# One decoder layer on one core: w_ada in pairs of blocks, the seam of the channel mixing in a pinned order, and operand tiles placed alike modulo 512 bytes

## The chip, the core and the metric

The kernel runs on one core of a Trainium2 chip. The metric is device time in microseconds (us) of one execution; of several executions the median is given. TensorE (PE) multiplies matrices, VectorE (DVE) and ScalarE (ACT) work on elements, GpSimd (POOL) does elementwise work and issues some transfers, and SyncE's queue (SP) issues most transfers (DMA). Matmul results stand in PSUM, everything else that an engine reads stands in SBUF, whose 128 partitions each hold a row of bytes; an address below is a byte offset in such a row.

## The reference

One conditioned decoder layer, in float32, on 1024 tokens of width 1024:

```
mod = silu(c) @ w_ada + b_ada                 # 1024 x 6144: shift1 scale1 gate1 shift2 scale2 gate2
h   = rmsnorm(x)*norm1_g*(1+scale1) + shift1
p   = h @ w_in                                # 5384 columns: r, wd, k, v, ad, gd | q, k, v, f | two gates
ya  = rwkv7(p ...); yb = forgetting_attention(p ...)
x   = x + gate1 * ((sigmoid(ga)*(ya@w_o_rwkv) + sigmoid(gb)*(yb@w_o_fox)) @ w_out)
h2  = rmsnorm(x)*norm2_g*(1+scale2) + shift2
x   = x + gate2 * (square(relu(h2 @ w_ff1)) @ w_ff2)      # 1024 -> 4096 -> 1024
y   = rmsnorm(x)*final_g
```

Every matrix product is computed to nearly float32 accuracy: an operand is split into a rounded part (`hi`, made by ACT) and the rest (`lo`, made by DVE as operand minus `hi`), and TensorE adds hi·hi, lo·hi and hi·lo. Such a product of 128x128 by 128x512 is three matmuls.

## The kernel before

The program is written engine by engine in Python; a scheduler orders the instructions of each engine ahead of time, by its own cost estimates, and inserts the semaphore waits. Tiles come from pools; a tile with a tag waits until the last reader of the tile that held the tag's buffer before it is done. Pools stand on the left or the right side of SBUF, and a pool that is opened where another was closed waits in the same way. `tc.keep_in_program_order` keeps an instruction in the order of the program on its engine, and `tc.issue_after(i)` lets instructions be put into the order only behind `i`.

**The start** (0 to 87 us). `x` comes in eight tiles of 128 tokens, all loaded first. `normalise(g)` squares four of them on ACT and scales them, the first four on DVE, the last four on ACT. scale1 and shift1 are 2 x 8 blocks of 128 numbers: `ada_load(k)` brings block k of both (two transfers of 0.5 MB, a run of 512 bytes per row of w_ada, three buffers), and `ada_sum(k)` multiplies row j by silu(c)[j] and adds up: three of the eight row groups on POOL, five on DVE, and a last sum over partitions on PE (matmuls of one column, `gp<-ones,acc`), which DVE turns into `gs`. `modulate(k)` transposes the 128 columns k of all eight `x` tiles on PE (`xp`), and ACT and DVE make `hhi`, `hlo` of them. `products(k)` then adds k's part to the first three projections, 18 matmuls of 128x512: `wa` (decay and in-context-lr columns), `r0` and `k0`. The order written is: `x`, wa block 0, the three weights, block 1; then k = 0 to 7, with sum and transposes one block ahead.

**The middle** (87 to 930 us) is the two mixers; the change does not touch it. **p_out** (930 to 1023 us) is the product with w_out, 384 matmuls of 128x512 `p_out<-h_wo,hhi` and the like (L1181 to L1192), with the residual and second norm.

**Channel mixing, up** (to 1351 us): w_ff1 goes in 16 pairs of columns; each pair is a 2x2 block product done in the 7 products of Winograd's form of Strassen's scheme, of 12 matmuls each. The operands made of h2 (`B11`, `B21`, `B22`, `T1` to `T4`) stay; those made of w_ff1 (`uwhi/uwlo`, `S1` to `S4`, `A22`) are made anew for each pair from a load `ur` (L1114). The results are squared, summed (`f_sum`) and written to a DRAM buffer `f_d`, in the seven combinations that the down product needs.

**Channel mixing, down** (1345 to 1670 us): 4 groups of 7 steps, 48 matmuls each. Step s takes one of the seven from `f_d` (`dA`, split into `dh` and `fl`) and one combination of four blocks of w_ff2 (`B11`, `B12`, `B21`, `B22`, scaled by gate2; split into `wh` and `wl`). Even and odd steps use two sets of four PSUM banks, `y` and `x`. `prepare(s+1)` makes the operands of the next step and `loads(s+3)` issues the transfers three steps ahead; `evict` adds a PSUM bank to the output sums `acc`.

**The seam** is the place where up ends and down begins. Step 0's operands (`da`, `db`, made to `dh`, `dl`) are prepared during the last pair, and its matmuls start before the last pair's `T4` product. Those of step 1 (A11, B11) need buffers of the pools `fr` and `fp`, which open only when the pools of the up stage are closed:

```
for name in ("S1", "S2", "S4"):
    f_sum(NPAIR - 1, name)
for stack in (hx[2], hx[0], dax, hx[1], mix):
    stack.close()
psum_pools(x=(4, 512), y=(4, 512))
with pool(name="fr", bufs=1, side="right") as fr, pool(name="fp", bufs=1) as fp:
```

In the order that results, DVE scales B22 (`B_0_11641` below), makes `fl` of step 1's dA (`dA_11633`) and only then scales B11 (`B_0_11634`); the split of B11 (ACT `wh`, L1099; DVE `wl`, L1100) and with it step 1 wait for that. The loads go in the order dA3, B22, dA1, B11, dA2, B12.

## Time and profile before

| | us |
|---|---|
| median of 3 runs (1678.31 to 1679.96) | 1678.47 |
| profiled execution | 1680.21 |
| its span, first to last instruction | 1678.5 |
| PE busy in the span | 1591.5 (95%) |
| DVE busy | 1132.0 (67%) |
| ACT busy | 730.7 (44%) |
| POOL busy | 357.9 (21%) |

The mean granted clock of TensorE over the profiled execution is 0.991 of full speed. Matmul times in a row are of a pipelined engine: one 128x512 matmul is shown with 0.39 us, but the next starts about 0.23 us after it. The distance from start to start (the pitch) is therefore what a matmul costs on a busy PE. In the chain of waits a piece "x48" is 48 instructions in a row on one engine, and its length over 48 is their pitch.

### The profile page before, as it was taken

To read this page: it belongs to the slowest core of one execution; us is meant where nothing else is said; L and a number is where in the kernel's file an instruction comes from. 1 tells how busy PE (TensorE), PEld (TensorE's weight loads), DVE (VectorE), ACT (ScalarE), POOL (GpSimd) and SP (SyncE) were. 2 spreads that over 40 slices of the span, in tenths; PEclk is the share of its full clock that TensorE was granted. 3 is DMA by queue.
4 is the path that set the end of the run, shared out by engine and by line. 5 is a ranking of instruction groups with operands and counts; after the bars stand their busy time and mean duration, and the time that the engine had idled before them with its cause. 6 is when DMAs were issued, how large, how long until landed. Compare 5 with 4: busy or idle time off the path is not lost.

```text
span 1678.5 us, 21911 instructions
## 1 busy us (share of the span) xinstructions
PE 1591.5 (95%) x8293; PEld 1274.8 (76%) x8293; DVE 1132.0 (67%) x1685; ACT 730.7 (44%) x1138; POOL 357.9 (21%) x362
## 2 busy tenths in 40 slices
PE   2989999999999999999999999999999979999997
PEld 1767777777777878888887787777777858888886
DVE  5777665657655736665737656975555579899978
ACT  5455343535454623332333234655545534433334
POOL 4310000899990011221110000122211110000000
PEclk9999999999999999999999999999999989999999
DMA  8525456422223178778767431344444474364422
GB/s 242 149 79 161 127 152 155 113 63 63 70 60 117 32 213 262 231 242 230 239 207 237 152 113 51 139 150 154 144 160 150 158 288 161 120 220 158 168 75 101
DMA packets 217111, 256.24 MB, mean 153 GB/s; under 512 B 30097, under 2 KB 156330, under 8 KB 216878
## 3 DMA queue, kind: packets, MB, share of 16 engines
q1 hardware_dynamic: 204094, 209.99, 41.3%
q0 software_dynamic: 12704, 44.57, 6.9%
q8 instruction: 65, 1.06, 0.3%
q14 instruction: 40, 0.33, 0.1%
q10 hardware_dynamic: 208, 0.28, 0.0%
HBM read 178.16 MB, written 72.45 MB: 149 GB/s over the span
## 4 chain that ended last, share of the span: by engine, by line
PE 70%; DVE 10%; DMA 7%; ACT 5%; issue 3%; SPq 0%; DVEq 0%; ACTq 0%
PE x L1221 18%; PE y L1221 11%; PE p_gb L41 5%; PE p_out L41 5%; PE p_ga L41 3%; PE p_ob L41 2%; PE p_fv L41 2%; DMA ur<-in_w_ff 2%; PE my L41 2%; PE p_fk L41 2%; PE p_fq L41 2%; PE z L1221 2%; PE p_v L41 2%; PE yv L41 2%; PE tp L825 2%
## 5 line engine op out<-in xcount | busy, mean ns | idle before, releaser
L1410 ACT CAST dh<-dA 128x1024 fp32r<-128x1024 f32 x54 | 56.4, 1046 | 139.9 <-PE x L1221 72.2
L1221 PE MATMUL x<-wh,dh 128*128 128x512 f32 x256 | 102.1, 399 | 9.4 <-ACT wh L1099 9.4
L645 POOL TENSOR_TENSOR dg<-dg,inv 128x62 f32<-128x62 f32 (+30 forms) x62 | 100.2, 1616 | 4.8
L1221 PE MATMUL x<-wl,dh 128*128 128x512 f32 x256 | 100.9, 395 | 0.0
L1221 PE MATMUL x<-wh,fl 128*128 128x512 f32 x256 | 100.1, 391 | 0.0
L644 POOL TENSOR_TENSOR inv<-dg 128x62 f32<-128x62 f32 (+30 forms) x62 | 92.8, 1497 | 4.9
L1591 DVE TENSOR_TENSOR fl<-dA,dh 128x1024 fp32r<-128x1024 f32 x54 | 65.1, 1218 | 16.1 <-ACT dh L1410 10.3
L1221 PE MATMUL y<-wh,dh 128*128 128x512 f32 x176 | 69.4, 394 | 0.0
L1221 PE MATMUL y<-wl,dh 128*128 128x512 f32 x176 | 68.6, 393 | 0.5 <-DVE wl L1100 0.5
L1221 PE MATMUL y<-wh,fl 128*128 128x512 f32 x176 | 68.3, 388 | 0.0
L829 DVE TENSOR_TENSOR pl<-tp,ph 128x512 fp32r<-128x512 f32 (+1 forms) x80 | 49.1, 631 | 24.9 <-ACT ph L828 24.6
L1221 PEld LDWEIGHTS x<-wh,dh 128*128 128x128 f32 x256 | 48.8, 191 | 19.6 <-ACT wh L1099 9.8
L885 DVE CUSTOM_DVE_ANT_0 pt<-s,cb 128x512 f32<-128x512 f32 (+2 forms) x64 | 36.4, 584 | 37.5 <-PE s L41 36.6
L887 ACT ACTIVATE pt<-pt,sm 128x128 f32<-128x128 f32 (+3 forms) x64 | 49.5, 775 | 24.4 <-DVE sm L885 23.4
L707 POOL TENSOR_TENSOR sw<-sbd,wcs 64x256 f32<-64x256 f32 x28 | 22.9, 816 | 167.9 <-DVE sbd L708 137.7
L1245 ACT ACTIVATE ff<-ff 128x512 f32<-128x512 f32 x48 | 30.3, 632 | 64.9 <-DVE ff L1331 29.5
L1221 PEld LDWEIGHTS x<-wl,dh 128*128 128x128 f32 x256 | 48.3, 189 | 12.0 <-DVE wl L1100 0.5
L1221 PEld LDWEIGHTS x<-wh,fl 128*128 128x128 f32 x256 | 48.6, 190 | 10.7
L828 ACT CAST ph<-tp 128x512 fp32r<-128x512 f32 (+1 forms) x80 | 41.6, 543 | 29.1 <-PE tp L825 27.2
L1236 POOL DMA_DIRECT2D f_d<-ff x48 | 25.9, 540 | 125.5 <-ACT ff L1246 121.1
L825 PE MATMUL tp<-ident,pt 128*128 128x128 f32 x288 | 49.6, 282 | 2.1 <-ACT pt L887 1.7
L41 PE MATMUL p_out<-h_wo,hhi 128*128 128x512 f32 x128 | 50.8, 397 | 0.6 <-ACT h_wo L1056 0.6
(586 smaller groups left out, 4932.6 us busy)
## 6 DMA issues: line engine op xcount, KB each, us to landing
dA<-f_d SPq DMA_DIRECT2D x27, 1024.0 KB
aw<-in_w_ada SPq DMA_DIRECT2D x32, 512.0 KB
ur<-in_w_ff SPq DMA_DIRECT2D x30, 512.0 KB
B<-in_w_ff SPq DMA_DIRECT2D x15, 1024.0 KB
f_d<-ff POOLq DMA_DIRECT2D x48, 256.0 KB, 4.3
wa<-in_w_ada SPq DMA_DIRECT2D x16, 512.0 KB
sc_d<-scb SPq DMA_DIRECT2D x16, 512.0 KB
sct<-sc_d SPq DMA_DIRECT2D x16, 512.0 KB
```

The lines of the kernel that those rows point to most:

```text
L41: PE.matmul(o, l, r, start=start, stop=stop)
L644: POOL.tensor_tensor(tv, dg[:, 0:s, s : s + 1].broadcast_to([P, s, m]), dg[:, s : s + 1, s + 1 :].broadcast_to([P, s, m]), ALU.mult)
L645: POOL.tensor_tensor(dg[:, 0:s, s + 1 :], dg[:, 0:s, s + 1 :], tv, ALU.add)
L825: PE.transpose(tp[:, x * P : (x + 1) * P], pr[b][:, t * P : (t + 1) * P], ident)
L828: ACT.copy(ph[:, 0:w_], tp[:, 0:w_])
L829: DVE.tensor_tensor(pl[:, 0:w_], tp[:, 0:w_], ph[:, 0:w_].bitcast(F32), ALU.subtract)
L885: DVE.tensor_tensor_reduce(pt[:, c0:c1], sv, cb[:, c0:c1], -0.125, low, ALU.add, ALU.min, st_[:, x : x + 1])
L887: ACT.activation(pt[:, 0:n], pt[:, 0:n], AF.Exp, bias=low, scale=-1.0, accum_out=ls[:, b : b + 1])
L1221: PE.matmul(o, l, r, start=start, stop=stop, skip_group_check=True)
L1245: ACT.activation(f, f, AF.Relu)
L1410: ACT.copy(hs[i], src[:, 2 * i : 2 * i + 2])
L1591: DVE.tensor_tensor(fl[:, sl], src[:, sl], f32(hs[i_]), ALU.subtract)
```

## The change

Three parts. **The start**: w_ada is loaded in four pairs of blocks (two transfers of 1 MB each, runs of 1 KB per row, two buffers), the first pair between `x` tiles 3 and 4, and the weights in the order r0, k0, second pair, wa. POOL sums nothing. For k below 3 all eight row groups are summed on PE (16 matmuls of one column, `gp<-cact,wa`, which need no DVE), from k = 3 all eight on DVE, in a pinned order. The transposed blocks 0 and 1 are split by halves of the tokens. The products of r0 and k0 for k = 0 and 1 come first, those of wa for them behind block 2's transposes. In `normalise(1)` DVE scales two of the four tiles. The 13 small loads of `second_columns` go to POOL's queue and are issued at k = 3.

**The seam**: the loads of B11 and dA1 stand right behind the one of `db`, B11 is scaled on DVE before the last pair's sums S1, S2 and S4, step 1's operands have buffers of their own (`wh_second` in a new pool `fq`, `dh_second` in the buffer of tag `dr`), and the evictions of step 0 and the preparations of steps 2 to 5 are put behind step 1's split. The load of dA3, which uses the buffer of tag `dr` too, is issued behind step 0's products. The scaling of `db` by gate2, which only step 6 needs, leaves the seam.

**Placement**: three tiles that nothing reads shift what is allocated behind them. In the program as built, the offsets modulo 512 of the left operands (`h_wo`, `uwhi`, `wh` and the like) stay at 352; those of the tiles on the right side go from 416 to 352, of p_out's pool `dp` from 480 to 352, and of `fp` from 0 to 352. The operands of the p_out, up and down stages then all stand at 352 modulo 512; those of `p_fv` and `p_ga` in the middle do so before and after.

```
+    def behind(done):
+        return tc.issue_after(done[-1].ins) if done else nullcontext()
...
+            wa = st.tile([P, KT, 2, 2 * P], F32, tag="wa", name=f"wa{q}", bufs=2)
+            SP.dma_start(wa[:, :, 0, :], w_ada[:, :, D + 2 * q * P : D + 2 * (q + 1) * P])
+            SP.dma_start(wa[:, :, 1, :], w_ada[:, :, 2 * q * P : 2 * (q + 1) * P])
...
-                if g:
+                if g and t % 2:
                     ACT.activation(xs[t], xs[t], AF.Copy, scale=r)
...
-            rest = wa[:, c0:].rearrange("p k i n -> p k (i n)")
-            POOL.tensor_tensor(rest, rest, cact[:, c0:].unsqueeze(2).broadcast_to([P, NPOOL, 2 * P]), ALU.mult)
-            for j in range(c0 + 1, KT):
-                POOL.tensor_tensor(wa[:, c0], wa[:, c0], wa[:, j], ALU.add)
...
+            if k < 3:
+                for i in range(2):
+                    for j in range(KT):
+                        mm(gp[:, i : i + 1], wa[:, j, i, :], cact[:, j : j + 1], j == 0, j == KT - 1)
+            else:
+                acc = st.tile([P, 2, P], F32, tag="acc", name=f"acc{k}", bufs=3)
+                with behind(sums):
+                    DVE.tensor_scalar(acc, wa[:, 0], cact[:, 0:1], None, ALU.mult)
+                    for j in range(1, KT):
+                        last = DVE.scalar_tensor_tensor(acc, wa[:, j], cact[:, j : j + 1], acc, ALU.mult, ALU.add)
+                sums.append(last)
...
+        modulate(0)
+        products(0, (1,))
+        first_tile(2, "k0", raw_k, wp, False)
+        products(0, (2,))
+        modulate(1)
+        products(1, (1, 2))
+        ada_sum(2)
+        modulate(2)
+        first_tile(0, "wa", raw_wa, st, False)
+        products(0, (0,))
+        products(1, (0,))
+        for k in range(2, KT):
...
-            if k == 5:
+            if k == 3:
                 omu, hbase, kmh, kmo = second_columns()
...
+    dpp.tile([P, 16], F32, name="dpp_rest")
...
+    px.tile([P, 96], F32, name="px_rest")
...
+        if second:
+            h = dpr.tile([P, 4, 512], F32R, name="dh_second", tag="dr", bufs=1)
+            hs = [h[:, 2 * i : 2 * i + 2] for i in range(2)]
...
+    load_b(0, "B11")
+    load_a(1)
+    early = [scale_b("B11")]
+    with behind(early):
+        for name in ("S1", "S2", "S4"):
+            f_sum(NPAIR - 1, name)
...
+        fp.tile([P, 88], F32, name="fp_rest")
...
+            if g == 0 and i == 1:
+                h_ = fq.tile([P, 4, 512], F32R, name="wh_second")
...
+            early.append(split(h_, l_, src))
...
+            with behind(early if 0 < s < 6 else []):
+                prepare(s + 1)
...
+                with behind(early if s == 0 and t else []):
+                    for half, d in to:
+                        evict(o, t + 4 * half, d, s > 0)
...
+            if s == 0:
+                loads(3)
```

What this does to the order of the instructions is shown at three places. The first is PE's program at the start; `gp` are the sums of w_ada, `xp` the transposes, `p_r`, `p_k` and `p_wa` the products. Before:

```order
L123 MATMUL vt_a<-ident,vr_a 128x32
L41 MATMUL gp_208<-ones,acc_202 128x1
L41 MATMUL gp_208<-ones,wa_148 128x1
L41 MATMUL gp_208<-ones,acc_202 128x1
L41 MATMUL gp_208<-ones,wa_148 128x1
L302 MATMUL xp_0_222<-ident,x_132 128x128
```

Changed:

```order
L41 MATMUL gp_180<-cact,wa_140 128x1 x8
L306 MATMUL xp_0_248<-ident,x_132 128x128
L306 MATMUL xp_0_248<-ident,x_134 128x128
L306 MATMUL xp_0_248<-ident,x_136 128x128
L41 MATMUL gp_180<-cact,wa_140 128x1 x8
L306 MATMUL xp_0_248<-ident,x_138 128x128
L41 MATMUL gp_180<-cact,wa_140 128x1 x16
L306 MATMUL xp_1_256<-ident,x_143 128x128
L41 MATMUL p_r_245<-hhi,wh_r_241 128x512
```

Block 0's 16 sums and block 1's 16 stand ahead of the second half's transposes and of the first product.

The second place is SP's queue at the seam, from the load of step 0's `db` on. Before:

```order
L1405 DMA db_11488<-in_w_ff 128x4x512
L1503 DMA dA_11639<-f_d 128x4x512
L1509 DMA B_0_11641<-in_w_ff 128x4x512
L1503 DMA dA_11633<-f_d 128x4x512
L1509 DMA B_0_11634<-in_w_ff 128x4x512
L1503 DMA dA_11631<-f_d 128x4x512
L1509 DMA B_0_11632<-in_w_ff 128x4x512
L1503 DMA dA_11716<-f_d 128x4x512
```

(`dA_11639` is dA3, `B_0_11641` B22, `dA_11633` dA1, `B_0_11634` B11, `dA_11631` dA2, `B_0_11632` B12, `dA_11716` dA4.) Changed:

```order
L1429 DMA db_11494<-in_w_ff 128x4x512
L1532 DMA B_0_11615<-in_w_ff 128x4x512
L1526 DMA dA_11614<-f_d 128x4x512
L1526 DMA dA_11612<-f_d 128x4x512
L1532 DMA B_0_11613<-in_w_ff 128x4x512
L1532 DMA B_0_11722<-in_w_ff 128x4x512
L1526 DMA dA_11726<-f_d 128x4x512
L1526 DMA dA_11798<-f_d 128x4x512
L1526 DMA dA_11724<-f_d 128x4x512
```

B11 (`B_0_11615`) and dA1 (`dA_11614`) moved to the front, and dA3 (`dA_11724`) from the first place to one behind dA2, B12, B22, dA4 and dA5 (`dA_11612`, `B_0_11613`, `B_0_11722`, `dA_11726`, `dA_11798`).

The third is DVE at the seam; `ff`, `fs` and `ft` are the last pair's results and sums, `acc` the evictions of steps 0 and 1. Before:

```order
L1517 TENSOR_TENSOR db_11488<-db_11488,gt_5349 128x2048
L1321 TENSOR_TENSOR ff_15_11503<-x_11469,ff_15_11503 128x512
...
L1345 TENSOR_TENSOR ft_11602<-ff_15_11596,ft_11602 128x512
L1559 TENSOR_TENSOR acc_11669<-y_0_0_11656,gt_5349 128x512
L1559 TENSOR_TENSOR acc_11684<-y_0_1_11671,gt_5349 128x512
L1559 TENSOR_TENSOR acc_11699<-y_0_2_11686,gt_5349 128x512
L1559 TENSOR_TENSOR acc_11714<-y_0_3_11701,gt_5349 128x512
L1517 TENSOR_TENSOR B_0_11641<-B_0_11641,gt_5349 128x2048
L1591 TENSOR_TENSOR fl_11647<-dA_11633,dh_0_11643 128x1024
L1591 TENSOR_TENSOR fl_11647<-dA_11633,dh_1_11644 128x1024
L1517 TENSOR_TENSOR B_0_11634<-B_0_11634,gt_5349 128x2048
L1100 TENSOR_TENSOR wl_1_11653<-B_0_11634,wh_1_11652 128x2048
```

Changed:

```order
L1345 TENSOR_TENSOR ff_15_11509<-x_11475,ff_15_11509 128x512
L1535 TENSOR_TENSOR B_0_11615<-B_0_11615,gt_5353 128x2048
L1369 TENSOR_TENSOR fs_11587<-ff_15_11528,ff_15_11509 128x512
L1369 TENSOR_TENSOR ft_11621<-fs_11587,ff_15_11446 128x512
L1369 TENSOR_TENSOR ft_11621<-ff_15_11602,ft_11621 128x512
L1123 TENSOR_TENSOR wl_1_11659<-B_0_11615,wh_second 128x2048
L1640 TENSOR_TENSOR fl_11654<-dA_11614,dh_second 128x1024 x2
L1608 TENSOR_TENSOR acc_11675<-y_0_0_11662,gt_5353 128x512
L1608 TENSOR_TENSOR acc_11690<-y_0_1_11677,gt_5353 128x512
L1608 TENSOR_TENSOR acc_11705<-y_0_2_11692,gt_5353 128x512
L1608 TENSOR_TENSOR acc_11720<-y_0_3_11707,gt_5353 128x512
L1640 TENSOR_TENSOR fl_11732<-dA_11612,dh_0_11728 128x1024
```

The scaling of `db` is gone from here, B11's (`B_0_11615`) stands behind the last result `ff`, and `wl` and `fl` of step 1 stand ahead of step 0's four evictions instead of behind them and the scaling of B22.

## Rows read from the trace of the kernel before

**Rows 1.** The page: granted clock of TensorE in 40 slices, tenths.
```profile
PEclk9999999999999999999999999999999989999999
```

**Rows 2.** Timeline of PE at the start: start, duration, instructions, idle before.
```profile
22.90 0.59 PE L41 MATMUL gp<-ones,acc 128*128 128x1 f32 x2 [14.20 <-DVE acc L285]
...
24.63 1.95 PE L302 MATMUL xp<-ident,x 128*128 128x128 f32 x8
29.32 1.22 PE L41 MATMUL p_wa<-hhi,wh_wa 128*128 128x512 f32 x2 [2.75 <-ACT hhi L304]
...
39.87 1.01 PE L41 MATMUL gp<-ones,acc 128*128 128x1 f32 x4 [4.60 <-DVE acc L285]
...
58.59 0.50 PE L41 MATMUL gp<-ones,acc 128*128 128x1 f32 x4
...
64.05 0.50 PE L41 MATMUL gp<-ones,acc 128*128 128x1 f32 x4
...
86.81 0.47 PE L41 MATMUL p_v<-hhi,wh_v 128*128 128x512 f32 x1 [0.16 <-DVE wa_t L446]
```

**Rows 3.** Timeline of DVE, the same stretch.
```profile
35.66 4.16 DVE L285 SCALAR_TENSOR_TENSOR acc<-wa,cact,acc 128x256 f32<-128x256 f32 x4
...
41.75 2.05 DVE L285 SCALAR_TENSOR_TENSOR acc<-wa,cact,acc 128x256 f32<-128x256 f32 x4
```

**Rows 4.** Timeline of ACT, the same stretch.
```profile
12.44 1.04 ACT L262 ACTIVATE jk<-x 128x1024 f32<-128x1024 f32 x1
```

**Rows 5.** Busy time by engine, granted clock, DMA rate of two stretches.
```profile
0.00:22.90 22.90, 0.28 (x1) 0.18 (x1) 10.71 (x30) 16.75 (x26) 5.97 (x23) 1.00 0.97 297
22.90:45.05 22.15, 13.71 (x47) 10.66 (x47) 16.02 (x19) 7.33 (x9) 11.80 (x9) 0.87 0.77 191
```

**Rows 6.** Chain of waits, p_fv: start, length, what.
```profile
276.04 10.89 PE p_fv L41 x48
```

**Rows 7.** Chain of waits, p_out.
```profile
986.02 24.00 PE p_out L41 x104
```

**Rows 8.** Chain of waits, down steps.
```profile
1449.93 10.99 PE x L1221 x48
```

**Rows 9.** Chain of waits, one pair of the up stage.
```profile
1170.17 2.98 PE x L1221 x12
...
1175.44 6.67 DMA ur<-in_w_ff
...
1189.14 0.69 DVE ff L1321
```

**Rows 10.** Chain of waits, last pairs and step 0's loads.
```profile
1303.91 2.80 PE x L1221 x12
...
1333.79 6.38 DMA db<-in_w_ff
```

**Rows 11.** Timeline of PE at the seam.
```profile
1359.76 0.40 PE L1221 MATMUL y<-dl,dh 128*128 128x512 f32 x1
1369.54 0.80 PE L1221 MATMUL x<-wh,dh 128*128 128x512 f32 x1 [9.38 <-ACT wh L1099]
...
1374.02 0.39 PE L1221 MATMUL x<-wh,fl 128*128 128x512 f32 x1
...
1385.42 0.50 PE L1221 MATMUL y<-wl,dh 128*128 128x512 f32 x1 [0.52 <-DVE wl L1100]
```

**Rows 12.** Timeline of DVE at the seam.
```profile
1345.36 2.29 DVE L1517 TENSOR_TENSOR db<-db,gt 128x2048 f32<-128x2048 f32 x1
...
1360.80 2.28 DVE L1517 TENSOR_TENSOR B<-B,gt 128x2048 f32<-128x2048 f32 x1
1363.00 2.35 DVE L1591 TENSOR_TENSOR fl<-dA,dh 128x1024 fp32r<-128x1024 f32 x2
1365.27 2.28 DVE L1517 TENSOR_TENSOR B<-B,gt 128x2048 f32<-128x2048 f32 x1
```

**Rows 13.** Timeline of ACT at the seam.
```profile
1367.59 1.90 ACT L1099 CAST wh<-B 128x2048 fp32r<-128x2048 f32 x1 [6.58 <-DVE B L1517]
```

More of the change, by code (lines that the diff above doesn't have):

```diff
@@ L1 @@
 import math
-from contextlib import ExitStack
+from contextlib import ExitStack, nullcontext
 import concourse.bass as bass
@@ L213, in second_columns @@
             one("bsh2", ada[3]),
-        ], SP)
+        ], POOL)
         nmu = 14
@@ L229, in build @@
         rtmp = st.tile([P, 16], F32, name="rtmp")
-        xs, was, gs, firsts = [], [], [], []
+        xs, was, gs, gps, sums, firsts = [], [], [], [], [], [None] * 3
         def x_load(t):
@@ L303, in modulate, with h_split, products @@
                 ACT.activation(hr[:, sl], xp, AF.Identity, bias=gs[k][:, 1:2], scale=gs[k][:, 0:1])
-            ACT.copy(hhi[:, k, :], hr)
-            DVE.tensor_tensor(hlo[:, k, :], hr, hhi[:, k, :].bitcast(F32), ALU.subtract)
-        def products(k):
-            for w, o in firsts:
+                if k < 2:
+                    h_split(k, hr, sl)
+            if k >= 2:
+                h_split(k, hr, slice(0, S))
+        def h_split(k, hr, sl):
+            ACT.copy(hhi[:, k, sl], hr[:, sl])
+            DVE.tensor_tensor(hlo[:, k, sl], hr[:, sl], hhi[:, k, sl].bitcast(F32), ALU.subtract)
+        def products(k, which=(0, 1, 2)):
+            for w, o in [firsts[i] for i in which]:
                 for a, b in ((0, hhi), (1, hhi), (0, hlo)):
@@ L1405, in start_down, with hi_halves @@
             SP.dma_start(nx[x], src)
-    def hi_halves(s, src):
-        hs = [wp.tile([P, 2, 512], F32R, name=f"dh{s}_{i}", tag=("whi", "wlo")[s % 2], bufs=2) for i in range(2)]
+    def hi_halves(s, src, second=False):
+        if second:
+            h = dpr.tile([P, 4, 512], F32R, name="dh_second", tag="dr", bufs=1)
+            hs = [h[:, 2 * i : 2 * i + 2] for i in range(2)]
+        else:
+            hs = [wp.tile([P, 2, 512], F32R, name=f"dh{s}_{i}", tag=("whi", "wlo")[s % 2], bufs=2) for i in range(2)]
         for i in range(2):
@@ L1522, in down_b @@
             if i == 1:
-                scale_b("B11")
+                if g:
+                    scale_b("B11")
             elif i == 2:
```

154 lines of the change are left out of this document (76 added, 78 removed).

## The prediction

> **What bounds the kernel now.** I read the page first: TensorE's granted clock is at nine tenths or more in all 40 slices (42 us each) but one, the 33rd, from 1343 us on [rows 1]: that is the seam, and little time is lost by a slow clock elsewhere. The timeline of PE then shows where it waits. At the start nothing runs on it before the first sum of w_ada at 22.90 us, 14.20 us of that behind DVE's sums; then 2.75 and 4.60 us more, and between 22.9 and 45.05 the mean clock is only 0.87 [rows 2, 5]. Later blocks of the k loop follow each other every 5.46 us (58.59 to 64.05). At the seam PE stands still for 9.38 us and comes back at half clock: from 1369.54 to 1374.02 the matmuls are far apart, then 0.23 us [rows 11]. Everywhere else near the change PE is gapless, and what a matmul costs is its pitch: 10.89/48 = 0.2269 in p_fv, 24.00/104 = 0.2308 in p_out, 10.99/48 = 0.2290 in the down steps [rows 6 to 8]. The up stage is the exception: the chain of one pair runs over PE, ACT and DVE to a load of 6.67 us, which waits for buffers of the pair before, and a pair takes 19.7 us (1170.17 to 1189.14 + 0.69) [rows 9]. There PE sits on the chain with one product of 12 matmuls (2.98 us) only.
>
> **The change, part by part.** All sums are made against the profiled execution (1680.21 us; span 1678.5, so 1.7 lie around it). The median is 1.74 below it, which I take off at the end.
>
> *The start.* Out go POOL's sums and, for k below 3, DVE's. DVE's four sums of 128x256 take 4.16 us beside POOL (1.04 each) and 2.05 alone (0.51 each) [rows 3], so those that stay from k = 3 on cost 8 x 0.51 = 4.1, with the split and small work of a block about 5.4 of DVE, just what PE needs for one (5.46). That is a tie, not a wait. In come 3 x 16 one-column matmuls on PE. Before, 4 sums took 24.63 - 22.90 = 1.73 us, 0.43 each, at the lower clock [rows 2], so 16 are 6.9 us there, and some 3 at full clock.
>
> When can they begin? The transfers bring 297 GB/s on average up to 22.9 us [rows 5]. Four x tiles and the first half of pair 0 are 3.1 MB, there at 10.6 us; the second half at 14.1, x4 to x7 at 21.2, r0 and k0 at 24.7, pair 1 at 32. So block 0's sums end near 17.5 and its first transposes near 18; block 1's 16 sums fill PE until about 25, while nothing else could run. ACT squares x4 to x7 (1.04 each [rows 4]) as they land, to 22.5, behind the first half's `hr`; with the root and two scalings on each engine they are ready near 26. The products of r0 and k0 can run from 27 to 31; I take 29. From there to the state "k = 0 and 1 complete, block 2 transposed" are 36 products, 16 sums and 16 transposes: at full clock about 36 x 0.233 + 2.9 + 1.6 = 12.9 us, at the lower one twice that. I take a low clock for the first 4.5 us, as at the seam [rows 11], so 44. The rest is block 2's products (18 x 0.233 = 4.2) and five blocks at 5.46: 75.5, where p_v's first matmul starts at 86.81 before, 0.16 after the loop's end [rows 2]. **-11**, bounds -4 (products from 31 at the low clock throughout k = 0 to 2) and -15 (from 27 at full clock).
>
> Moving second_columns to POOL's queue I put at nothing: POOL has no sums left to do, and what these 13 loads bring is read after the loop, 20 us behind their issue. If they came later than that, each microsecond would be one on the path.
>
> *p_out.* 384 matmuls. The unalike pitch is 0.2308 over the last 104 and somewhat more before; the alike one in p_fv 0.2269 [rows 6, 7]. 384 x 0.004 = **-1.6**, bounds 0 (if placement is not the reason) and -2.
>
> *Up.* Three of the seven products of a pair have operands that stand apart, 2.80 us for 12 [rows 10], 2.72 at p_fv's pitch. If PE bound the stage, 16 pairs with 36 such matmuls would give 16 x 3 x 0.08 = 3.8. But the chain passes PE in one product only, whose rows are PE's pace less than that of ACT, DVE and the load [rows 9]; I take 0.05 a pair for 14 pairs, and 0.24 for each of the last two, which load nothing more: **-1.2**, bounds 0 and -4.
>
> *The seam.* Before, B11 is scaled at 1365.27 because the scaling of B22 (2.28) and step 1's `fl` (2.35) go first on DVE, then ACT makes `wh` until 1369.5 [rows 12, 13]. After, B11's load is issued when T1's last product is read: counted back from step 0's end at 1360.0 [rows 11] over its 48 matmuls, T4's 12 and three products of 2.80 [rows 10], near 1337.4. It stands behind `db`, whose landing took 6.38 [rows 10], and lands by 1346 at the latest, by the same duration and some 2 us for sharing the queues. DVE is free of the scaling of `db` (2.29 at 1345.36) and scales B11 behind `ff`, from about 1347.3 to 1349.6. ACT squares the last pair's results until about 1351.7, makes `wh_second` (1.90) by 1353.6 and `dh_second` (half the columns in half the time, twice) by 1355.6, DVE `wl` and `fl` (2.3 each) by 1358.1 to 1360.4 as the halves come. Step 0 ends at 1360.0 as before, and step 1's first matmuls need only `wh_second` and `dh_second`: it starts without a wait. What the pinned order queues behind B11's scaling on DVE are the sums S1, S2 and S4, and behind step 1's split the four evictions of step 0; those are wanted by step 2 only, at 1371.
>
> What is late next: step 2's `wl` waits for DVE, which clears step 1's evictions first; before, the same wait was 0.52 [rows 11], I take 1.2. And there is a new wait. `dh_second` sits in the buffer that dA3 needs, so SP can load dA3 only when step 1's last product has read it, near 1371; landing takes some 6.4, then come `dh` (2.1), `fl` (2.3), T (2.28) and `wh` (1.9), one behind the other, to 1385.5. Step 2 ends at 1383, so step 3 starts 2.5 late and loses some 0.8 more for `wl`: it ends near 1397.1 where before it ended at 1406.0 (1449.93 less four steps of 10.99 [rows 8]). **-8.7**; bounds -4 (dA3 lands 5 us later, PE comes back at half clock) and -11 (the whole wait and the half clock are gone).
>
> *Down.* 24 steps of 48 are left, 10.99 each; at p_fv's pitch 10.89: **-2.4**, bounds 0 and -3 [rows 6, 8]. DVE has the time: its work in a step is below PE's.
>
> Sum: -11 - 1.6 - 1.2 - 8.7 - 2.4 = -24.9, which makes 1655.3 of 1680.2 and, less 1.74, 1653.6. I say **1654**. The bounds together reach from -8 to -35; not all come out at one end, and I take 1643 to 1670.
>
> **The rivals.**
> - *The start is bound by something else* (13%). Transfers before 22.9 us already keep the DMA engines busy at 0.97 [rows 5], and nothing in the change brings fewer bytes; if r0 and pair 1 land later than I reckon, or DVE's tie with PE tips, only 4 of the 11 are won: 1661. For it speaks the busy share, against it that the order now brings first what PE needs first.
> - *Placement does nothing* (13%). The pitches differ between stages [rows 6 to 8], but stages differ in more than placement. Without p_out, up and down the sum is -19.7, so 1659. For it speaks that PE shows no idle time between these matmuls, so nothing visible makes the difference; against it, that 0.2269 stands where the offsets are equal and 0.229 to 0.233 where they are not. The Trainium skill would have it this way (SBUF — State Buffer, "Who interferes with whom"): PE and ACT never wait for another user of SBUF, and only the ports that VectorE and GpSimd share make one engine slow another. By that rule the offsets of PE's own operands would bring nothing, the time being this rival's; no row here tests it, since no stage of before ran at two placements.
> - *Placement shortens the up stage in full* (5%): 2.8 more, 1651. Against it speaks the load in every pair's chain.
> - *The seam's wait moves to step 3* (12%). The price named above grows: dA3 lands late, PE idles 5 us or more and comes back at half clock, as it did from 1369.54 to 1374.02. Then the seam gives 3 to 4: 1659.
> - *Slower* (6%). One-column matmuls leave TensorE at the lower clock, and it stays there through the k loop. A block then costs 18 x 0.43 + transposes and sums 2.4, about 10.2 instead of 5.46; the state that I put at 44 comes at 55. With n of the six blocks at that level the start loses 4.7 n; it gives back all that the other parts win (13.9 with the sum above) from n = 3 on and is slower than can be missed from n = 4. With all six it is 55 + 6 x 10 = 115, 28 more than before, and the time 1693. For it speaks that the clock was low at 22.9 to 45 us around such sums; against it, that it rose there, and at the seam after 4.5 us of products.
>
> **How the numbers follow.** The forecast has 51%, with a range of its own from 1648 to 1660; the rivals that end faster have 13, 13, 5 and 12%, and slower has 6. Changes within 0.2% (3.4 us, about what a measurement of this kernel can tell from no change) need nearly all parts to fail at once, and come from the tail of the first and fourth rivals together: 4%. That leaves 89% for faster and 7% for slower.
>
> **What would show it.** In the profile of the changed kernel: PE's first matmul near 11 us and products from 27 to 31; p_v's first product near 75; a pitch of 0.227 in p_out and 10.89 for a down step; pairs of the up stage still 19.7 us apart; no wait at step 1, one of 1 to 2 us at step 2 and one of 2 to 3 at step 3, named after `wh` or `dh` behind dA3's load. Wrong would be: an unchanged down step (placement), a step 1 that still waits for `wh_second`, or a granted clock of half through blocks 2 to 7.

## The result and the profile after

The changed kernel takes 1665.47 us (median of 3 runs, 1665.38 to 1665.49) where the kernel before takes 1678.47: a ratio of 0.9907, with a 95% interval of 0.9884 to 0.9930. It is faster, and inside the predicted range of 1643 to 1670, but 11.5 us above the 1654 forecast and outside the 1648 to 1660 that the forecast gave for itself. So the sign was right and the sum was not, and the question is which term failed.

Both traces are cut at the same events of TensorE's timeline: the first matmul of p_v (the end of the k loop), the first of `s` (attention), the first of p_out, the first product of the up stage, the end of its last `z`, and the last matmul of all. All are profiled executions, in us.

| stretch | before | after | difference | forecast |
|---|---|---|---|---|
| start to p_v | 86.81 | 86.13 | -0.68 | -11 |
| p_v to the first s | 225.12 | 228.90 | +3.78 | 0 |
| s to p_out | 576.84 | 577.01 | +0.17 | 0 |
| p_out to the up stage | 132.93 | 131.71 | -1.22 | -1.6 |
| up stage to the last z | 307.43 | 300.71 | -6.72 | -1.2 |
| last z to the end (seam, down) | 340.53 | 329.72 | -10.81 | -8.7 - 2.4 = -11.1 |

(Behind the last matmul another 0.8 us is lost, which no row holds.) The first row is the failure. The timeline of PE after, at the start, answers to [rows 2] (a sum of 8 one-column matmuls shows as x16):

```profile
12.34 3.55 PE L41 MATMUL gp<-cact,wa 128*128 128x1 f32 x16 [4.64 <-DMA wa<-in_w_ada]
...
20.32 6.98 PE L41 MATMUL gp<-cact,wa 128*128 128x1 f32 x32 [0.18 <-DVE gs L297]
30.21 0.48 PE L306 MATMUL xp<-ident,x 128*128 128x128 f32 x1 [2.90 <-DVE x L274]
30.34 0.77 PE L41 MATMUL p_r<-hhi,wh_r 128*128 128x512 f32 x1
...
35.35 0.63 PE L41 MATMUL p_k<-hhi,wl_k 128*128 128x512 f32 x1
35.78 0.63 PE L41 MATMUL p_r<-hlo,wh_r 128*128 128x512 f32 x1
...
39.41 4.82 PE L41 MATMUL gp<-cact,wa 128*128 128x1 f32 x32 [0.43 <-ACT hr L307]
...
45.04 0.78 PE L41 MATMUL p_r<-hhi,wh_r 128*128 128x512 f32 x1
...
46.47 0.63 PE L41 MATMUL p_r<-hhi,wl_r 128*128 128x512 f32 x1
46.90 0.63 PE L41 MATMUL p_r<-hlo,wh_r 128*128 128x512 f32 x1
...
52.65 0.50 PE L41 MATMUL gp<-ones,acc 128*128 128x1 f32 x4
...
86.13 0.47 PE L41 MATMUL p_v<-hhi,wh_v 128*128 128x512 f32 x1 [0.16 <-DVE wa_t L468]
```

The sums do start early (12.34 for 22.90), and the first product comes at 30.34. But the state that I put at 44 us comes at 52.65, and by then nothing is left of the lead. Two things stand in the rows. First, PE waits 2.90 us for x4 to x7, and these were late for a reason in DVE's and ACT's order, here DVE and then ACT:

```profile
27.35 0.28 DVE L296 TENSOR_SCALAR gs<-gp,bsc,vc_a 128x1 f32<-128x1 f32 x1 [7.08 <-PE gp L41]
...
29.40 1.42 DVE L274 TENSOR_SCALAR x<-x,rs 128x1024 f32<-128x1024 f32 x2
```
```profile
20.36 0.78 ACT L307 ACTIVATE hr<-xp,gs 128x512 f32<-128x512 f32 x1 [8.15 <-DVE gs L297]
...
24.83 1.04 ACT L267 ACTIVATE jk<-x 128x1024 f32<-128x1024 f32 x1
```

DVE stands 7.08 us before block 1's `gs`, which waits for PE's 16 sums, and the scaling of x4 to x7 is queued behind it. ACT stands 8.15 us before block 0's `hr`, and the squares of x4 to x7 are queued behind that. Second, the clock: it falls to half during block 2's sums (39.41 to about 44.1) and is back only near the end of block 1's products (48.65). Busy time of PE, PEld, DVE, ACT and POOL, then granted clock, DMA share and GB/s, after:

```profile
38.00:44.00 6.00, 5.57 (x39) 5.33 (x38) 0.00 (x0) 2.47 (x4) 0.00 (x0) 0.82 0.00 0
44.00:50.00 6.00, 6.00 (x23) 5.00 (x23) 4.90 (x10) 1.71 (x2) 0.00 (x0) 0.61 0.00 0
```

Before the trace's first entry of the clock, 38.41 us here, this view reads 1.00 for want of an entry; the products there stand 0.43 us apart (35.35 to 35.78), as they do at half clock (46.47 to 46.90), so the lower level (1.2 GHz) held from the first product on. The 1.00 in [rows 5], and part of its 0.87, are no reading either.

The second row of the table was in no term of mine. PE waits in front of p_fv, where before it did not [rows 6]:

```profile
279.47 0.50 PE L41 MATMUL p_fv<-hhi,wh_fv 128*128 128x512 f32 x1 [2.58 <-DVE sgd L471]
```

The seam came out as worked out. The timelines of PE and of ACT after, answering to [rows 11, 13]:

```profile
1356.19 1.07 PE L1245 MATMUL x<-wh_second,dh_second 128*128 128x512 f32 x4
1367.07 0.39 PE L1245 MATMUL y<-wh,dh 128*128 128x512 f32 x1
1370.22 0.50 PE L1245 MATMUL y<-wl,dh 128*128 128x512 f32 x1 [1.17 <-DVE wl L1123]
1380.26 0.50 PE L1245 MATMUL x<-wh,dh 128*128 128x512 f32 x1 [0.64 <-ACT wh L1122]
1382.72 0.50 PE L1245 MATMUL x<-wl,dh 128*128 128x512 f32 x1 [0.33 <-DVE wl L1123]
```
```profile
1347.76 1.89 ACT L1122 CAST wh_second<-B 128x2048 fp32r<-128x2048 f32 x1
1349.56 1.99 ACT L1438 CAST dh_second<-dA 128x1024 fp32r<-128x1024 f32 x2
```

Step 1 starts without a wait, and step 2 waits 1.17 us for `wl` (forecast 1.2). Step 3 waits 0.64 and 0.33 where I had 2.5 and 0.8. The chains of waits after, of a down step, of one pair of the up stage and of p_out, answer to [rows 8, 9, 7]:

```profile
1435.61 10.88 PE x L1245 x48
```
```profile
1160.53 2.72 PE y L1245 x12
...
1173.71 6.75 DMA ur<-in_w_ff
```
```profile
999.89 22.21 PE p_out L41 x98
```

The products of the up stage in which PE does not wait now take 2.72 for 12 (2.73 to 2.80 before), a down step 10.88 (10.99), a matmul of p_out 22.21/98 = 0.2266 (0.2308).

### The profile page after: what moved, and what is told of

The parts are those of the page before. It is cut to its first block, busy times and chain, and to the rows that moved or that the text cites. A ratio compares the mean times of both kernels' runs of the same rounds, so it can differ in the third digit from the quotient of the medians.

```text
span 1663.8 us, 22023 instructions
## 1 busy us (share of the span) xinstructions
PE 1596.7 (96%) x8373; PEld 1289.1 (77%) x8373; DVE 1115.9 (67%) x1689; ACT 728.9 (44%) x1138; POOL 336.4 (20%) x352
## 4 chain that ended last, share of the span: by engine, by line
PE 70%; DVE 12%; DMA 9%; ACT 5%; issue 3%; SPq 0%; DVEq 0%; ACTq 0%
PE x L1245 15%; PE y L1245 9%; PE p_out L41 5%; PE p_gb L41 4%; PE p_ga L41 4%; PE p_fv L41 3%; DMA ur<-in_w_ff 2%; PE p_fk L41 2%; PE p_fq L41 2%; PE my L41 2%; PE p_ob L41 2%; PE p_v L41 2%; PE p_r L41 2%; PE yv L41 2%; PE p_k L41 2%
## 5 line engine op out<-in xcount | busy, mean ns | idle before, releaser
L1245 PE MATMUL x<-wh,dh 128*128 128x512 f32 x240 | 93.6, 390 | 1.3 <-DVE acc L1602 0.7
L1245 PE MATMUL x<-wh,fl 128*128 128x512 f32 x240 | 93.4, 389 | 0.0
L1245 PE MATMUL x<-wl,dh 128*128 128x512 f32 x240 | 93.0, 390 | 0.3 <-DVE wl L1123 0.3
L1245 PEld LDWEIGHTS x<-wh,dh 128*128 128x128 f32 x240 | 45.0, 188 | 11.4 <-ACT dh L1438 1.1
L1245 PEld LDWEIGHTS x<-wh,fl 128*128 128x128 f32 x240 | 45.0, 188 | 9.4
L41 PE MATMUL p_gb<-hhi,wl_gb 128*128 128x512 f32 x128 | 51.4, 402 | 0.1
L41 PE MATMUL p_ga<-hhi,wh_ga 128*128 128x512 f32 x128 | 51.1, 400 | 0.0
```

What stands on the lines that cost most here:

```text
L41: PE.matmul(o, l, r, start=start, stop=stop)
L1245: PE.matmul(o, l, r, start=start, stop=stop, skip_group_check=True)
```

## The experiments

Twelve experiments ran, in four groups that each shared a chip with runs of the kernel before: e1 to e4, e5 to e8, e9 to e11, e12. Ratios are to the kernel before on the same chip. On these chips single runs of one kernel scatter by 5 to 13 us, so stretches of the profiled executions, cut as above, say more than medians; each column is of one execution all the same:

| kernel | to p_v | p_v to s | s to p_out | p_out | up | z to end | median | ratio, 95% interval |
|---|---|---|---|---|---|---|---|---|
| e1_banks | 85.73 | 227.04 | 577.80 | 132.98 | 305.45 | 329.15 | 1665.22 | 0.9914 [0.9898, 0.9930] |
| e2_old_start | 86.51 | 226.39 | 582.36 | 130.24 | 306.14 | 328.38 | 1666.99 | 0.9927 [0.9911, 0.9942] |
| e3_no_pads | 85.32 | 229.71 | 579.44 | 134.18 | 303.51 | 333.87 | 1670.76 | 0.9958 [0.9943, 0.9974] |
| e4_old_seam | 84.03 | 226.97 | 583.88 | 131.50 | 302.73 | 337.93 | 1673.93 | 0.9962 [0.9947, 0.9977] |
| e5_after_again | 84.04 | 227.59 | 578.63 | 133.12 | 305.88 | 328.68 | 1669.61 | 0.9939 [0.9921, 0.9956] |
| e6_sum2_dve | 83.08 | 225.80 | 578.41 | 130.60 | 305.57 | 328.24 | 1663.84 | 0.9916 [0.9896, 0.9937] |
| e7_norm_first | 82.41 | 226.90 | 581.84 | 132.32 | 303.64 | 328.83 | 1664.56 | 0.9911 [0.9894, 0.9929] |
| e8_norm_sum2 | 78.89 | 229.48 | 578.73 | 132.38 | 305.69 | 327.87 | 1665.10 | 0.9913 [0.9895, 0.9932] |
| e9_sum1_dve | 76.98 | 227.83 | 578.27 | 131.70 | 307.21 | 327.65 | 1663.69 | 0.9889 [0.9864, 0.9913] |
| e10_warm | 76.89 | 228.63 | 579.91 | 130.84 | 302.29 | 328.99 | 1661.60 | 0.9878 [0.9854, 0.9903] |
| e11_norm_sum2_banks | 77.88 | 228.24 | 574.46 | 130.23 | 306.11 | 328.86 | 1658.17 | 0.9862 [0.9835, 0.9889] |
| e12_all | 76.92 | 224.55 | 575.31 | 132.14 | 305.75 | 327.78 | 1655.16 | 0.9861 [0.9837, 0.9885] |

**e1_banks: the wait before p_fv.** By the program's assignment of PSUM, the new order of the start turns round which pair of banks each later tile gets: p_gd comes to lie on banks 0 and 1, which p_fv takes next, and so p_fv waits for the eviction `sgd`. The edit gives p_fv other banks.

```diff
-    psum_pools(pj=(2, 512), s=(3, 512), tp=(2, 512), yv=(1, 512))
+    psum_pools(tp=(2, 512), pj=(2, 512), s=(3, 512), yv=(1, 512))
```

> Only the PSUM pools of the stage behind the k loop are laid out in another order, so that p_fv's tiles no longer take the banks of p_gd. Theory: p_fv's first matmul waits 2.58 us for DVE's sgd in the changed kernel because it takes p_gd's bank, and comes back at the lower clock; without that the middle gives back about 3 us: 1662 to 1663.5 for the changed kernel's 1665.5, and no wait of over 0.3 us at p_fv's first matmul. Rival: the wait is for sgd's data or for DVE's order and stands as before: 1665.5.

The cause of the wait is shown, the gain is not: the median, 1665.22, is what the rival had. p_fv starts without a wait, but one of 2.32 us comes back in front of p_fq, where the kernel before had 2.00 and the changed kernel has none. The timeline of PE in e1:

```profile
305.64 0.47 PE L41 MATMUL p_fq<-hhi,wh_fq 128*128 128x512 f32 x1 [2.32 <-DVE kl L816]
```

From p_v to s it takes 227.04. The kernels with the new start and the old pools take 225.80 to 229.71, the three with the new pools 224.55 to 228.24. At most 1 to 2 us lie in it, and the scatter is as large.

Most of that scatter, and most of the 3.8 us in the first table, is the clock. The timeline of PE in e6 has the same wait as after; the windows behind it are the whole stretch from p_v to `s` of before, after and e6, in this order, with the columns as above:

```profile
274.98 0.50 PE L41 MATMUL p_fv<-hhi,wh_fv 128*128 128x512 f32 x1 [2.58 <-DVE sgd L471]
```
```profile
86.81:311.92 225.11, 214.83 (x1143) 165.82 (x1144) 150.21 (x177) 93.00 (x129) 18.91 (x14) 0.99 0.50 141
86.13:315.03 228.90, 217.79 (x1144) 168.09 (x1144) 146.47 (x177) 93.16 (x129) 20.94 (x17) 0.98 0.48 139
83.08:308.88 225.80, 214.69 (x1143) 165.84 (x1144) 147.26 (x177) 93.04 (x129) 19.50 (x15) 0.99 0.49 141
```

PE stands idle for 10.28, 11.11 and 11.11 us, so all the waits together, p_fv's 2.58 against the 2.00 at p_fq among them, cost 0.8 of the 3.8; the other 3.0 are the same matmuls at a lower mean clock, and e6 has the waits without it. Over all fourteen traces this stretch goes with the mean clock: 224.55 to 225.80 us at 0.992 (before, e6, e12), 226.39 to 228.24 at 0.985 (e1, e2, e4, e7, e11), 227.59 to 229.48 at 0.978 (after, e5, e8, e9, e10), 229.71 at 0.970 (e3). Why it falls more often in one execution than in another is not shown.

**e2_old_start: the start against the rest.** The whole block from the loads of x and w_ada to the end of the k loop is that of the kernel before (blocks of w_ada one by one, three of eight rows summed on POOL, five on DVE).

```diff
-        def ada_load(q):
-            wa = st.tile([P, KT, 2, 2 * P], F32, tag="wa", name=f"wa{q}", bufs=2)
+        def ada_load(k):
+            wa = st.tile([P, KT, 2, P], F32, tag="wa", name=f"wa{k}", bufs=3)
...
-            if k < 3:
-                for i in range(2):
-                    for j in range(KT):
-                        mm(gp[:, i : i + 1], wa[:, j, i, :], cact[:, j : j + 1], j == 0, j == KT - 1)
+            POOL.tensor_tensor(rest, rest, cact[:, c0:].unsqueeze(2).broadcast_to([P, NPOOL, 2 * P]), ALU.mult)
```

> The changed kernel with the start (w_ada's blocks one by one, sums on DVE and POOL, loads on the old queues) of the kernel before. Theory: the new start wins 0.7 us of its own and costs 3 to 4 in the middle, since it turns round which bank pair each later tile gets; so this kernel is faster than the changed one, about 1662 to 1663, and p_fv's first matmul waits for nothing. Rival: the new start is worth what its own stretch shows (0.7 us) or more, and the middle's 3 us come from the other parts: 1666 to 1669.

Neither came out whole. The time, 1666.99, is the rival's (1666 to 1669) and not my 1662 to 1663, but the wait before p_fv is gone, as the theory had it. p_v starts at 86.51, against 84.03 to 85.73 in the three kernels with the new start on the same chip; p_v to s takes 226.39 against 226.97 to 229.71. So the new start wins 0.8 to 2.5 us and gives 0.6 to 3.3 back behind the loop, 0.6 where the mean clock is the same (e1, e4). The total is not lower than that of e1, which shares all the rest but the order of the PSUM pools.

**e3_no_pads: placement by itself.** Three tiles that nothing uses are left out; no instruction changes.

```diff
-    dpp.tile([P, 16], F32, name="dpp_rest")
...
-    px.tile([P, 96], F32, name="px_rest")
...
-        fp.tile([P, 88], F32, name="fp_rest")
```

> The changed kernel without its three filler tiles (dpp_rest, px_rest, fp_rest), so that the operands of p_out, of the up stage's three products and of the down steps stand apart modulo 512 bytes again; nothing else is touched. Theory: placement alone shortens the matmul's pitch; without it p_out gives back 1.2 us, the up stage 5 to 6 and the down steps 2.4: 1674 to 1675.5, a down step of 10.99, 12 matmuls of the up stage at 2.75 to 2.80 and a p_out pitch of 0.231. Rival: placement does nothing, the pitches of the changed kernel come from the order of the work: 1665.5. Second rival: only p_out and down depend on it, and the up stage's 6.7 us come from the order: 1669.

Placement sets the pitch, and "placement does nothing" is dead; the time, 1670.76, is nearer to the second rival's 1669 than to the theory's 1674 to 1675.5. The chains of waits in e3, of one pair of the up stage, of p_out and of down steps (the last line late in the stage):

```profile
1180.76 2.76 PE y L1243 x12
1183.52 2.80 PE x L1243 x12
1186.32 2.80 PE y L1243 x12
1189.12 2.80 PE x L1243 x12
1191.92 2.75 PE z L1243 x12
```
```profile
999.92 26.10 PE p_out L41 x113
```
```profile
1433.12 10.99 PE y L1243 x48
...
1598.83 11.20 PE x L1243 x48
```

All the pitches of before are back [rows 7, 8, 10]: 2.80, 26.10/113 = 0.2310, 10.99. From 1587 us on the down steps of this trace even take 11.20, though modulo 512 their operands stand as before; that stays open. By stretches, p_out costs 134.18 (130.2 to 133.1 in the traces with fillers), and seam and down 333.87 (327.7 to 329.7 in those with fillers and the new seam). The up stage costs 303.51, in the middle of 300.7 to 307.2: there the shorter pitch buys nothing that can be seen.

What it is about the placement is not shown, and "operands alike modulo 512" is not enough. In the program as built, `hhi`, `uwhi`, `T2` and `dh` stand at 352 in all three kernels; the tiles that move to 352 are `h_wo` (from 480 and 416), `S1` to `S4`, `A22`, `T1`, `T4` and `wh` (from 416), `wl` and `fl` (from 0), so the list of left operands under "The change" is not right. The `z` above multiplies `hhi` and `uwhi`, alike at 352 in e3 as after, and takes 2.75 for 2.72; the first `y` multiplies `T1` and `S1`, alike at 416 in e3, and takes 2.76. And in the down steps of before, `wh` and `fl` stand apart (416 and 0), yet the next matmul starts 0.226 us behind theirs, no later than after.

**e4_old_seam: the seam by itself.** B11 loaded and scaled where it was, step 1 without buffers of its own, the sums S1, S2, S4 in the old place, no pinned order; the placement stays.

```diff
-    early = [scale_b("B11")]
-    with behind(early):
-        for name in ("S1", "S2", "S4"):
-            f_sum(NPAIR - 1, name)
+    for name in ("S1", "S2", "S4"):
+        f_sum(NPAIR - 1, name)
...
-            if g == 0 and i == 1:
-                h_ = fq.tile([P, 4, 512], F32R, name="wh_second")
```

> The changed kernel with the seam of the kernel before: B11 loaded and scaled behind step 0's split, step 1 without halves of its own buffer, S1, S2 and S4 where they were, no pinned order; the operands stand alike as in the changed kernel. Theory: the seam's new order is worth what was forecast for it, 8.7 us, and the new waits (1.17 at step 2, 0.97 at step 3) belong to it: 1673.5 to 1675, with a wait of about 9 us before step 1. Rival: part of the 13 us by which step 1 starts earlier comes from the up stage's last pairs and not from the seam: 1669 to 1671.

From the last z to the end it takes 337.93, and 328.38 to 329.15 in e1 and e2 on the same chip: the seam is worth 8.8 to 9.6 us (forecast 8.7). The timeline of PE in e4 shows the old wait to the hundredth [rows 11]:

```profile
1369.07 0.80 PE L1245 MATMUL x<-wh,dh 128*128 128x512 f32 x1 [9.38 <-ACT wh L1122]
```

What is left against the kernel before, 340.53 - 337.93 = 2.6, is the down steps' pitch (forecast 2.4).

**e5_after_again: what varies.** No edit.

> The changed kernel itself once more, as the yardstick of the runs that share its chip, and for what varies from one profiled execution to the next. Theory: start, p_out, seam and down steps are set by the order and the pitch of PE and come out as before within 1 us each (p_v from 86, z's end to the last product 329 to 330); the up stage, which sits between PE's pace and a chain over DVE and a load, is the part that varies: 301 to 306 us from its first product to the last of z, so most of the 6.7 us that it gained in the first profile are not the change's. Rival: the up stage repeats its 300.7 us, and the gain is the placement's.

The up stage takes 305.88, not 300.71, while seam and down repeat to 1.04 us and p_out, 133.12 for 131.71, to 1.4. In the seven pairs of this trace that wait, PE stands before T4's product for DVE's `ff`. One such row, and the chain's products of 3.03, where the wait and the first matmul's lag are part of the 12:

```profile
1210.78 0.50 PE L1245 MATMUL x<-T4h,A22h 128*128 128x512 f32 x1 [0.45 <-DVE ff L1345]
```
```profile
1171.34 3.03 PE x L1245 x12
```

So with the shorter pitch a pair takes 19.05 to 19.2 us where PE is not kept waiting, and about 19.7 where it waits at the end of the chain over the load (6.67 to 6.75 us). In the first trace more pairs took the lower time, in e2 and e9 nearly all take 19.7; why a pair falls on one side or the other is not shown. Of the 6.7 us in the first table, this kernel can count on little. Its start, 84.04, is 2 us better than in the first trace, which my theory did not expect. The clock goes with it: from 38 to 50 us its mean is 0.72 in the first trace, e1 and e3, where p_v comes at 85.32 to 86.13, and 0.86 in e4 and e5, where it comes at 84.03 and 84.04.

**e6, e7, e8: why the start gave nothing.** e6 takes block 2's sums off PE:

```diff
-            if k < 3:
+            if k < 2:
```

e7 pins two orders, the squares of x4 to x7 ahead of block 0's `hr` on ACT, and their root and scaling ahead of block 1's `gs` on DVE:

```diff
+        done = normalise(1)
         ada_sum(0)
-        ada_sum(1)
+        with behind(done):
+            ada_sum(1)
         ada_load(2)
-        normalise(1)
...
-        modulate(0)
+        with behind(done[:1]):
+            modulate(0)
```

e8 has both.

> The changed kernel with block 2's sums on VectorE as those of the later blocks; blocks 0 and 1 keep theirs on TensorE. Theory: the 16 one-column matmuls of block 2 (39.41 to 44.08, 4.7 us) stand between the transposes of block 1 and its products and are followed by the lower clock (0.50 from 42 to 48); without them block 1's products begin near 40 and the loop's end comes 3 to 6 us earlier: p_v from 80 to 83. Rival: DVE, on the path there for the first tiles' splits, takes block 2's four microseconds of sums so late that PE waits for gs2 instead: p_v at 86 or later.

> The changed kernel with two orders pinned at the start: ACT squares x4 to x7 before it writes block 0's first half, and DVE's root and scaling of x4 to x7 stand ahead of block 1's gs. Theory: the x tiles lay ready and waited behind work that itself waited for block 1's sums on PE (gs of block 1 at 27.35 after 7.08 us idle); in this order they are scaled by 27.5, the first products start 2 to 3 us earlier, and p_v comes 2 to 4 us earlier, 82 to 84. Rival: the clock decides, since PE stays at the lower level until some microseconds of products have run, and the products only run as much earlier as the first one starts, with the same wait later for block 1's hhi: p_v at 85 to 86.

> Both edits of the two kernels before: the pinned order and block 2's sums on VectorE. Theory: the two do not share a cause, so their gains add: p_v at 77 to 81, and the time 5 to 9 us below the changed kernel. Rival: with both, DVE becomes the bound of the start (its sums of block 2, the splits of r0 and k0 and the scaling fall into the same 8 us), and p_v stays at 84 to 86.

p_v comes at 83.08, 82.41 and 78.89, for 84.04 (e5, same chip) and 86.13 (first trace). Against the first trace the gains are 3.05, 3.72 and 7.24: they add. Against e5 they are 0.96, 1.63 and 5.15, more than their sum. e7 alone still pays for the clock, as the same windows as above show, in e7 and then in e8.

```profile
38.00:44.00 6.00, 6.00 (x27) 5.71 (x27) 2.36 (x6) 1.44 (x2) 0.00 (x0) 0.50 0.02 6
44.00:50.00 6.00, 6.00 (x30) 4.91 (x29) 3.75 (x8) 2.09 (x3) 0.00 (x0) 0.93 0.62 202
```
```profile
38.00:44.00 6.00, 6.00 (x34) 4.89 (x32) 5.18 (x12) 2.75 (x4) 0.00 (x0) 1.00 0.58 149
44.00:50.00 6.00, 5.90 (x32) 4.47 (x31) 5.39 (x12) 3.69 (x5) 0.00 (x0) 1.00 0.44 139
```

With block 2's sums on PE (e7) the clock is half from 38 to 44; without them (e8) it does not fall there. So it is in all traces of the new start: from 38 to 50 us the mean is 0.72 or 0.86 in the six with these sums on PE (after, e1, e3, e4, e5, e7) and 1.00 in the six without (e6, e8 to e12). And the order did what it should: in e8 DVE scales x4 and x6 at 24.04, 5.36 us earlier than after, and the first product comes at 28.09. In e8 the wait that is left is for ACT's second `hhi`:

```profile
37.07 0.50 PE L41 MATMUL p_r<-hhi,wh_r 128*128 128x512 f32 x1 [1.61 <-ACT hhi L315]
```

The medians of the three lie within 1.3 us of each other and 4.5 to 5.8 below e5. The intervals of their ratios overlap with e5's: all three point the same way, but neither the size of one nor their order can be read from them.

**e9_sum1_dve: block 1's sums on DVE too.** `ada_acc` makes them on DVE in the idle time before block 0's `gs`; the pin ahead of block 1's `gs`, which waits for PE's sums no more, is left out.

```diff
-            if k < 3:
+            if k < 1:
...
+        ada_acc(1)
         ada_sum(0)
         ada_sum(1)
```

> The kernel with the pinned order and block 2's sums on VectorE, with block 1's sums on VectorE as well (only block 0 keeps its 16 one-column matmuls); DVE makes them ahead of block 0's gs, where it stands idle for 3.78 us. Theory: block 1's 16 sums hold PE from 20.5 to 27.5 ahead of the transposes of x4 to x7, which lie ready at 26.3; without them the first product comes at 26.7 to 27.2 instead of 28.1 and p_v at 77 to 78.5 (78.89 with block 1 on PE). Rival: an idle PE comes back at the lower clock for longer than one that ran one-column sums, and p_v stays at 78.5 to 81.

The first product comes at 27.39 and p_v at 76.98, close to the theory (26.7 to 27.2, and 77 to 78.5). The transposes of x4 to x7 now wait for nothing on PE but the data:

```profile
25.45 1.14 PE L317 MATMUL xp<-ident,x 128*128 128x128 f32 x3 [3.30 <-DVE x L274]
```

**e10_warm: the clock by itself.** Full matmuls whose result nothing reads fill PE's idle time.

```diff
+        def idle_work(n, after=None):
+            for _ in range(n):
+                with behind([after] if after else []):
+                    mm(jb, wj[:, 0:P], wj, True, True)
...
+        idle_work(6)
         ada_sum(0)
...
+                if k == 1:
+                    idle_work(18, end)
```

> The kernel before this one, with 6 matmuls of 128x512 ahead of block 0's sums and 18 behind block 1's, in the time in which PE waits for x4 to x7; what they write is read by nothing. Theory: the lower clock after the wait is what the first products pay (0.43 each until 35 us in the three kernels before); with PE kept busy by full matmuls up to 26.5 the products start at 0.23, about 14 of them are 0.2 shorter, and p_v comes 1.5 to 3 us earlier: 74.5 to 77. Rival: the first products wait for the splits of r0 and k0 on DVE whatever the clock, so p_v moves by less than 1 us, or the 18 end late and cost what they win.

The pitch does what the theory says and the time what the rival says. The timeline of PE in e10:

```profile
21.49 6.24 PE L41 MATMUL junkb<-wj 128*128 128x512 f32 x18
27.57 0.60 PE L319 MATMUL xp<-ident,x 128*128 128x128 f32 x4
27.92 0.47 PE L41 MATMUL p_r<-hhi,wh_r 128*128 128x512 f32 x1
28.23 0.39 PE L41 MATMUL p_r<-hhi,wl_r 128*128 128x512 f32 x1
...
29.96 0.50 PE L41 MATMUL p_k<-hhi,wh_k 128*128 128x512 f32 x1 [1.11 <-ACT wh_k L258]
```

The products start at 0.23 to 0.31 us apart instead of 0.42 to 0.60, and then PE waits 1.11 us for ACT's `wh_k`. p_v comes at 76.89 for 76.98. Half clock at the first products costs nothing that can be seen once ACT and DVE set the pace there.

**e11_norm_sum2_banks and e12_all: the pieces together.** e11 is e8 with the pools of e1, e12 is e9 with them; no new edit.

> The pinned order and block 2's sums on VectorE, and the PSUM pools behind the k loop in the other order: p_v at 79 as with the first two alone, no wait at p_fv's first matmul, and one of 2.0 to 2.3 at p_fq for DVE's kl in its place. Theory: the stretch from p_v to the first s is 1.5 to 2.5 us shorter than with the pools in the old order (227 for 228.9 to 229.5). Rival: p_fq's wait grows by what p_fv's was, and the stretch is the same.

> All that helped, in one kernel: pinned order, block 0's sums alone on TensorE, PSUM pools in the other order. Theory: p_v at 77 (as without the pools), from p_v to the first s 227 to 228.5, the rest as in the changed kernel: about 9 us less than the changed kernel at the start and 1 to 2 in the middle, so a ratio to the kernel before of 0.984 to 0.988. Rival: the start's gain is given back behind the loop, where PE then waits longer for DVE (3.88 us for wl_k at 96.93 in the run with the pools), and the ratio is 0.989 to 0.991.

e11 takes 228.24 from p_v to s for e8's 229.48, with 2.56 us before p_fq; the theory's 227 is not reached, and 1.2 us is within the scatter. e12 has the lowest time of all: 1655.16 us against 1679.40, a ratio of 0.9861 [0.9837, 0.9885], level with e11's 0.9862, where the changed kernel has 0.9907 and 0.9939. Its gain at the start is 9.2 us against the changed kernel's first trace and 7.1 against e5. The stretch behind the loop gives none of it back: 224.55 is the shortest of all, at the highest mean clock (0.992).

## Why the prediction came out as it did

- **Start, forecast -11, came -0.7 (0.8 to 2.5 against e2, on one chip).** The step that failed is the one from "products of r0 and k0 run from 27 to 31; I take 29" to "so 44". The first product came at 30.34, inside the bounds. Of the 22.3 us from there to the state "k = 0 and 1 complete" I had 15. The sums of block 2 were in my list as 2.9 us at full clock; they took 4.7 and sent the products of block 1 to half clock (e6 to e8). The low clock at the first products, too, was a term too small: I took 4.5 us of it, and it held for 8 (30.34 to 38.41). Of the 10.6 us between my 75.5 and p_v, these steps and the first product's 1.3 make 8.6; the other 2.0 lie behind, 33.5 us to p_v where I had 31.5, 1.02 of them a wait for `hhi`. And I let ACT square x4 to x7 "as they land", without asking what stood ahead of them in its order: they lay behind an instruction that waited for another engine, and so did their scaling on DVE (e7). Both causes are shown by taking them away: with both gone p_v comes at 78.89, with block 1's sums gone too at 76.98, where I had 75.5.
- **The first rival** named this place and a price near it (4 of the 11 won), but for the transfers' sake. They were not it: the DMA share is 0.00 from 38 to 44 us after, and the start gained 7 to 9 us without a byte less.
- **Slower rival.** Its mechanism is real: one-column matmuls do leave PE at the lower clock (0.72 or 0.86 from 38 to 50 us with block 2's on PE, 1.00 without). It holds for about one block of the six, not all, since the later blocks' sums are on DVE. I priced it by the block, but as a rival that counts from three blocks on, and left it out of the main sum, where a block of it (4.7) belonged.
- **A term that was missing: +3.8 behind the loop.** The changed order turned round the PSUM banks, and p_fv waits 2.58 us for `sgd`. e1 shows the cause of that wait, and that the remedy brings the one at p_fq back. Net, the waits of the stretch cost 0.8 us more than before; the other 3.0 are the lower mean clock of that one execution, which e6, with the same wait, does not have.
- **p_out -1.6, down -2.4: right** in size, and e3 shows that placement does it. p_out -1.22, and 384 x (0.2310 - 0.2272) = 1.46 by the mean pitches of e3 and of after; down 2.6 (e4). The reason that I gave, a matmul's own two operands standing alike or apart, is not shown, and e3's `z` and `T1` products speak against it as the whole reason. Here the measurement decides against what my second rival drew on. The Trainium skill (SBUF — State Buffer, "Who interferes with whom") gives TensorE two SBUF read ports, one for the moving operand and one for weight loads, and calls them independent. Where the tiles stand, with no instruction changed, moves the pitch from 0.2272 to 0.2310 in p_out and, by the mean over the stage, from 0.2268 to 0.2334 in the up stage's S2. Why is not shown by any run.
- **Up -1.2: right in mechanism, not to be measured in size.** The rival "in full" (3.8, so 2.6 more than my 1.2 and not the 2.8 that it says) seemed true in the first trace and more than true (6.7). Over the twelve traces in which the operands stand alike (the first one and all but e3), the stage takes 300.7 to 307.2, 304.8 in the mean, against 303.5 without fillers. PE's gain turned into waits for `ff`. So part of the total was luck: the first trace has the shortest up stage of all, and the same kernel on e5's chip took 1669.61, at the edge of my range.
- **Seam -8.7: right**, 8.8 to 9.6 by e4. (The two ends in my sum, 1406.0 and 1397.1, make 8.9.) Step 1 without a wait and 1.17 at step 2 came as forecast; step 3's wait was 1.0 in all where I had 3.3. The chain behind the landing of dA3 is there as forecast, `dh`, `fl`, T and `wh`, but it takes 7.6 us (1372.62 to 1380.21) for 8.6, since `fl` starts on the first half of `dh`; the rest of the difference was not followed up.

## What to carry to other kernels

Before pricing a moved operation by when its inputs land, read what stands ahead of it in its own engine's order and what that waits for; a single small instruction that waits for another engine holds everything behind it (8.15 us on ACT here). Price matmuls of one column by what the clock does to the products after them (a mean of 0.72 or 0.86 for 1.00 here), and put them on an idle engine where there is one. And a change of the order in which PSUM tiles are taken moves waits to places far from the edit, so look up which tile takes whose banks behind it. Before such a wait is made to pay for a longer stretch, compare PE's busy time as well: the same matmuls took 217.79 us in one execution and 214.69 in another.
